# The turned softmax blocks of a neighbourhood attention: from DRAM and back on GpSimd's queue, or straight from SBUF to SBUF on SyncE's

## The chip, the cores and the metric

The kernel runs on one core of a Trainium2 chip. The metric is the device time of one execution in microseconds (us). Three runs of the kernel before gave 1162.82, 1160.19 and 1152.91 us, with the median at 1160.19 us.

## The reference, cut to what matters

One layer of a hybrid block in float32: a half-step SwiGLU, a mixer with two branches, a second half-step SwiGLU. There are 512 tokens (8 rows of a grid of 64 columns), 1024 features, 16 heads of 64, and a feed-forward width of 2816. Branch B of the mixer is the attention that the change touches: every token attends to the 8 rows by 16 columns around it. The reference computes it in 4 blocks of 16 query columns with 32 key columns each, and masks what lies outside the window.

```python
x = x + 0.5 * swiglu(rmsnorm(x), w_ffn1_gu, w_ffn1_down)
p = rmsnorm(x) @ w_in          # [rglru x | gelu gate | q | k | v | merge gate A | merge gate B]
A = (rglru(conv(px)) + rglru_backward(conv(px))) * gelu(pg)
s = einsum('bnqhd,brnkhd->bhnqrk', q, k) + rel_pos_bias     # q and k normalized, window masked
B = einsum('bnqhrk,brnkhd->bnqhd', softmax(s), v)
x = x + (sigmoid(gA) * A + sigmoid(gB) * B) @ w_out
x = x + 0.5 * swiglu(rmsnorm(x), w_ffn2_gu, w_ffn2_down)
```

## The kernel before, in words

**Precision and weights.** Every operand of a large product is split in two rounded parts, a high and a low one, and each product is three matmuls (high weight by high data, high by low, low by high: L171 to L174, and L831 to L833 where tokens are the rows of the result). A weight chunk is 128 x 1024 numbers, 512 KB, and gives 24 such matmuls. `load_w` (L159) makes it ready: SyncE (SP) issues the load into `wraw` at L163, ScalarE (ACT) casts it to `wh` at L145 (every other chunk of some stages is cast by VectorE, DVE, at L147), and DVE subtracts to get `wl` at L148. There are three buffers of `wraw` and four of `wh` and `wl`. So the load of a chunk waits for the split of the chunk three before it, and the split waits until TensorE (PE) is through with the chunk four before it.

**Stages.** The first feed-forward layer takes the time to some 390 us, then come the projections, the recurrence on GpSimd (POOL) and DVE, and the attention; the second feed-forward layer starts near 780 us. The middle of the program is woven: while PE works through the weight chunks of V (`wqkv`), of the three gates (`wg`, 24 chunks, named wg0 to wg23 here) and of W_out (`wout`, 8 chunks), pieces of the attention are put between them. The program's order is the starting point, a scheduler then sets the order on each engine, and what stands under `tc.high_priority()` is moved ahead.

**The attention.** `heads(hf, ...)` (L889) handles one half of the heads, hf = 0 or 1, in four feature tiles fi of two heads each. For each tile:
- `start(fi)` turns q and k with PE and splits them.
- `scores(fi, n2s)` handles pairs n2 of the four column blocks: PE makes the scores (L943) into PSUM tiles named `aux` and `acc`, DVE adds the bias tile `bm` and finds the row's extreme in one pass (L963), ACT takes the exponent (L970), DVE inverts the row sums (L972) and scales (L975). The weights stand in tiles `p`.
- `ship(fi, n2)` (L978) turns the weights so that keys come to lie on the partitions. DVE transposes inside each 32 x 32 block (L984 and L985) into `pt`, a tile of 128 x 4 x 7 x 32, of which there are two buffers. What is left is to swap whole blocks across partitions: block row j of column group i has to become block row i of column group j. Before, POOL stores `pt` to device memory (`pd`, L987, one transfer of 448 KB) and then issues four loads of 112 KB into `PT` (L991), which has four buffers.
- `apply(fi)` (L994) multiplies PT by V in 16 matmuls of 128 x 64 weights (L1005), the first 8 on the PT of n2 = 0, the last 8 on that of n2 = 1, and ACT copies the result to `att` (L1015).

In the first half (hf 0) a step of the weave is one pair of column blocks: 8 steps, and an apply comes two steps behind its last scores. In the second half (hf 1) a step is a whole feature tile: 4 steps with two ships each. So there are 16 ships and 8 applies. They are numbered here in order: ships 0 to 7 belong to hf 0 (0 and 1 to its fi 0), ships 8 to 15 to hf 1; apply 0 to 3 of a half are its fi 0 to 3.

**What else stands on the queues there.** On POOL's queue also run the loads of the bias tiles (`bm`, L885) and, between the halves, the store of V and its gather into tiles `va`, `ve`, `vs` (L860 to L873). On SP's queue run the weight loads (L163) and, late, `load_pairs` and the residual (`xd`, L1098). Behind the attention, `att` enters the merge at L1084 and L1085 (pair times att, plus A); the result is split into `yh` and `yl`, which are the data of the W_out chunks, and these lead to the second feed-forward layer.

Of the kernel before, what the change touches and what calls it, by code (L numbers as in the profile page):

```python
# [9 lines left out]
F32 = mybir.dt.float32  # L10
# [6 lines left out]
P = 128  # L17
# [9 lines left out]
NCB, QC = 4, 16  # L27
# [64 lines left out]
def block_kernel(ctx: ExitStack, tc, a, out):  # L92
    nc = tc.nc
# [7 lines left out]
    dram = ctx.enter_context(tc.tile_pool(name="dram", bufs=1, space=bass.MemoryType.DRAM))  # L101
# [6 lines left out]
    def nm(s):  # L108
        uid[0] += 1
        return f"{s}_{uid[0]}"  # L110
# [147 lines left out]
    def sub(out_, in0, in1, neg=False):  # L258

        if neg:  # L260
            nc.vector.scalar_tensor_tensor(out_, in0, -1.0, in1, ALU.mult, ALU.subtract)
        else:
            nc.vector.tensor_tensor(out_, in0, in1, ALU.subtract)
# [617 lines left out]
    def bias(g):  # L881

        for hp in range(2):
            bms[g, hp] = tiny.tile([P, 640], F32, tag="bm", bufs=4, name=nm("bm"))
            ld = nc.gpsimd.dma_start(bms[g, hp], a["rpb"][g * 2 + hp])  # L885
            if g == 0:
                after(ld, mark["xr"])

    def heads(hf, raws, st):  # L889
# [9 lines left out]
        for w in range(2):  # L899
            for j in range(NCB):  # L900
                t = raws[w][j].rearrange("p (h d) -> p h d", d=HD)
# [5 lines left out]
        def start(fi):  # L907
            fs = slice(fi * P, (fi + 1) * P)
            pq, pk = aux_t(), aux_t()
            for j in range(NCB):  # L910
                hold(nc.tensor.transpose(pq[:, j * P : (j + 1) * P], raws[0][j][:, fs], ident))
            for j in range(NCB):
                hold(nc.tensor.transpose(perm(pk)[:, j], raws[1][j][:, fs], ident))
            rev = lambda t: t.rearrange("p (j t) -> p j t", j=NCB)[:, :, ::-1]
            fwd = lambda t: t.rearrange("p (j t) -> p j t", j=NCB)
            qh, ql, kh, kl = (big_t(F32R, n=n) for n in ("qh", "ql", "kh", "kl"))
            nc.scalar.activation(rev(qh), fwd(pq), AF.Copy, scale=gq8)
            with tc.high_priority():
                nc.vector.scalar_tensor_tensor(rev(ql), fwd(pq), gq8, rev(qh.bitcast(F32)), ALU.mult, ALU.subtract)
            nc.scalar.activation(kh, pk, AF.Copy, scale=gk)  # L920
            with tc.high_priority():
                mark["kl"] = nc.vector.scalar_tensor_tensor(kl, pk, gk, kh.bitcast(F32), ALU.mult, ALU.subtract)
            grid = lambda t: t.rearrange("p (r c) -> p r c", r=ROWS)
            qk[fi] = qh, ql, grid(kh), grid(kl)
# [53 lines left out]
        def ship(fi, n2):  # L978

            outer, inner = soft.pop((fi, n2))  # L980
            t = big.tile([P, NCB, 7, 32], F32, tag="pt", bufs=2, name=nm("pt"))
            sub = lambda b, n: b[:, : n * P].rearrange("p (q c i) -> p q c i", q=n, i=32)
            to = t.rearrange("p c q i -> p q c i")
            nc.vector.transpose(to[:, 4:], sub(outer, 3))  # L984
            nc.vector.transpose(to[:, :4], sub(inner, 4))  # L985
            d = dram.tile([P, NCB, 7 * 32], F32, tag="pd", bufs=4, name=nm("pd"))
            nc.gpsimd.dma_start(d, t.rearrange("p c q i -> p c (q i)"))  # L987
            PT = big.tile([P, NCB, 7, 32], F32, tag="PT", bufs=4, name=nm("PT"))
            for j in range(4):
                q = slice(j * 32, (j + 1) * 32)  # L990
                nc.gpsimd.dma_start(PT[:, j].rearrange("p q i -> p (q i)"), d[q].rearrange("i c x -> c i x"))  # L991
            PTs[fi, n2] = PT.rearrange("p a q i -> p q a i")

        def apply(fi, behind=None):  # L994
            pv = aux_t()
            for n in range(NCB):
                PT = PTs[fi, n // 2]
                for half in range(2):
                    if n in EDGE:
                        vt = V[hf, "single" if half else "own", n]  # L1000
                    else:
                        vt = V[hf, (KSTART[n] + half * QC) // 8]
                    for h2 in range(2):
                        q = 4 + (1 if half else h2 * 2) if n in EDGE else h2 * 2 + half
                        mm = nc.tensor.matmul(  # L1005
                            pv[h2 * HD : (h2 + 1) * HD, n * P : (n + 1) * P],
                            vt[:, (fi * 2 + h2) * HD : (fi * 2 + h2 + 1) * HD],
                            PT[:, q],
                            start=half == 0, stop=half == 1)
                        if behind is not None:  # L1010
                            after(mm, behind)
                            behind = None
            at = big_t(n="att")
            with tc.high_priority():
                nc.scalar.activation(  # L1015
                    at.rearrange("p (j t) -> p j t", j=NCB), pv.rearrange("p (j t) -> p j t", j=NCB)[:, :, ::-1], AF.Copy)
            att[hf * 4 + fi] = at
# [7 lines left out]
        for i in range(len(units) + LC):  # L1025
            behind = None
            if i < len(units):
                fi, n2s = units[i]
                behind = scores(fi, n2s)
            if i >= LC and 1 in units[i - LC][1]:  # L1030
                apply(units[i - LC][0], behind)
            if i < len(units):
                for n2 in n2s:
                    ship(fi, n2)
                if 0 in n2s:
                    if fi < 3:
                        start(fi + 1)
                    if hf * 4 + fi + 1 < KT:
                        bias(hf * 4 + fi + 1)
            yield  # L1040
            if phase[0] == "g":
                yield
                yield
# [4 lines left out]
    for hf in range(2):  # L1048
        st = tiny.tile([P, 2, NCB, 8], F32, tag="st", name=nm("st"))
        raws = [qk_raw(0, hf, st), qk_raw(1, hf, st)]  # L1050
        v_get(hf)
        lanes["att"].append(heads(hf, raws, st))
        phase[0] = "t1" if hf == 0 else "g"
# [146 lines left out]
```

## Time and profile before

| what | value |
| --- | --- |
| median of three runs | 1160.19 us (1152.91 to 1162.82) |
| the profiled execution, its own time | 1158.95 us |
| its span in the trace | 1157.1 us |
| mean granted clock of TensorE | 0.979 of full speed |
| busy: PE / DVE / ACT / POOL | 1108.7 / 813.8 / 581.1 / 162.7 us |
| moved by the transfers | 175.93 MB in 63588 packets |

How to read it: the span is the time from the first to the last instruction of one execution, and what lies around it (1.85 us here) is the start and the end. An engine's busy time is the sum of its instructions. A row of the timeline shows the start, the duration, the engine, the source line, what was written from what, and in brackets the idle time of the engine just before it with what ended it. A row of the stages shows, for a stretch of the span, its length and then each engine's busy time with its count of instructions (PE, PE's weight loads, DVE, ACT, POOL), then the granted clock, the busy share of the 16 DMA engines, and GB/s. A row of the transfers shows what was written from what, the issuing queue, the count, the KB of one, and the median of the us from issue to landing.

### The profile page before, as it was taken

The numbers are of one execution on the slowest core, as the hardware profiler recorded it, in microseconds if no ns is written. First come the engines' busy times: TensorE is split into PE (matmuls) and PEld (weight loads), VectorE is DVE, ScalarE is ACT, GpSimd is POOL, SyncE is SP. The second block draws the span as 40 slices with busy tenths as digits, with TensorE's granted clock in tenths as the row PEclk, the third lists the DMA queues.
The fourth block names the chain that finished last, engine by engine and source line by source line (L and its number), as shares of the span: only waits on it lengthen the run. The fifth ranks groups of instructions, "written<-read, shape, count | busy, mean of one in ns | idle before, by whom it ended". The sixth has DMA issues, their size and how long they took to land.

```text
span 1157.1 us, 17667 instructions
## 1 busy us (share of the span) xinstructions
PE 1108.7 (96%) x6811; PEld 980.1 (85%) x6811; DVE 813.8 (70%) x1295; ACT 581.1 (50%) x873; POOL 162.7 (14%) x267
## 2 busy tenths in 40 slices
PE   9999999999999999998884999699999999999998
PEld 7899999988888778886773887578999999998887
DVE  7877777775836869997463589737877777875552
ACT  8554545553625778765242254435754545464340
POOL 0000000000000531422343003310000000000000
PEclk9999999999999999999896999889999999999999
DMA  8566666632423883845654436648666666653420
GB/s 265 150 159 159 163 152 169 164 117 91 135 75 106 230 247 107 237 126 161 170 160 114 135 109 199 195 129 217 177 153 159 163 153 168 153 166 98 128 85 36
DMA packets 63588, 175.93 MB, mean 152 GB/s; under 512 B 15120, under 2 KB 18960, under 8 KB 63504
## 3 DMA queue, kind: packets, MB, share of 16 engines
q1 hardware_dynamic: 39744, 118.31, 31.9%
q0 software_dynamic: 23184, 56.24, 22.9%
q8 instruction: 53, 0.87, 0.3%
q10 hardware_dynamic: 576, 0.26, 0.1%
q14 instruction: 31, 0.25, 0.1%
HBM read 150.53 MB, written 15.73 MB: 144 GB/s over the span
## 4 chain that ended last, share of the span: by engine, by line
PE 78%; issue 7%; DMA 6%; POOL 4%; DVE 3%; ACT 1%; ACTq 0%; POOLq 0%; DVEq 0%
PE acc L312 30%; PE acc L172 8%; PE acc L174 8%; PE acc L173 8%; PE aux L312 5%; DMA pd<-pt 4%; PE aux L173 4%; PE aux L172 3%; PE aux L174 3%; POOL PT L991 2%; PE acc L831 1%; PE acc L832 1%; PE acc L833 1%; DMA PT<-pd 1%; PE aux L742 1%
## 5 line engine op out<-in xcount | busy, mean ns | idle before, releaser
L145 ACT ACTIVATE wh<-wraw 128x1024 fp32r<-128x1024 f32 (+3 forms) x224 | 220.6, 988 | 322.2 <-issue 92.4
L148 DVE TENSOR_TENSOR wl<-wraw,wh 128x1024 fp32r<-128x1024 f32 (+3 forms) x236 | 267.3, 1137 | 100.7 <-ACT wh L145 97.7
L312 PE MATMUL acc<-s,wh 128*128 128x256 f32 x1280 | 232.1, 283 | 0.0
L312 PEld LDWEIGHTS acc<-s,wh 128*128 128x128 f32 x1280 | 199.7, 192 | 0.0
L312 PE MATMUL acc<-s,wl 128*128 128x256 f32 x640 | 181.1, 283 | 0.0
L312 PEld LDWEIGHTS acc<-s,wl 128*128 128x128 f32 x640 | 122.9, 192 | 0.0
L172 PE MATMUL acc<-xh,wh 128*128 128x512 f32 x272 | 109.0, 401 | 0.0
L174 PE MATMUL acc<-xh,wl 128*128 128x512 f32 x272 | 107.4, 395 | 0.0
L173 PE MATMUL acc<-xl,wh 128*128 128x512 f32 x272 | 107.3, 395 | 0.0
L312 PE MATMUL acc<-xl,wh 128*128 128x256 f32 x320 | 90.6, 283 | 0.0
L312 PE MATMUL acc<-xh,wl 128*128 128x256 f32 x320 | 90.6, 283 | 0.0
L312 PE MATMUL acc<-xh,wh 128*128 128x256 f32 x320 | 90.5, 283 | 0.0
L831 PE MATMUL acc<-wh,xh 128*128 128x512 f32 x192 | 76.4, 398 | 0.0
L832 PE MATMUL acc<-wh,xl 128*128 128x512 f32 x192 | 75.4, 393 | 0.0
L833 PE MATMUL acc<-wl,xh 128*128 128x512 f32 x192 | 75.2, 392 | 0.0
L148 DVE TENSOR_TENSOR hl<-h,hh 128x512 fp32r<-128x512 f32 x88 | 57.2, 686 | 21.7 <-PE aux L173 21.4
L172 PE MATMUL aux<-hh,wh 128*128 128x512 f32 (+1 forms) x181 | 69.9, 386 | 0.0
L173 PE MATMUL aux<-hl,wh 128*128 128x512 f32 (+1 forms) x181 | 69.9, 386 | 0.0
L174 PE MATMUL aux<-hh,wl 128*128 128x512 f32 (+1 forms) x181 | 69.9, 386 | 0.0
L173 PE MATMUL acc<-hl,wh 128*128 128x512 f32 (+1 forms) x176 | 67.9, 386 | 0.0
L174 PE MATMUL acc<-hh,wl 128*128 128x512 f32 (+1 forms) x176 | 67.9, 386 | 0.0
L172 PE MATMUL acc<-hh,wh 128*128 128x512 f32 (+1 forms) x176 | 67.9, 386 | 0.0
(223 smaller groups left out, 2322.2 us busy)
## 6 DMA issues: line engine op xcount, KB each, us to landing
wraw<-wqkv SPq DMA_DIRECT2D x24, 512.0 KB, 5.0
wraw<-wg SPq DMA_DIRECT2D x24, 512.0 KB, 3.9
wraw<-w1d SPq DMA_DIRECT2D x22, 512.0 KB, 3.7
wraw<-w2s SPq DMA_DIRECT2D x22, 512.0 KB, 4.2
pair<-w2s SPq DMA_DIRECT2D x22, 512.0 KB, 5.0
wraw<-w2d SPq DMA_DIRECT2D x22, 512.0 KB, 3.6
wraw<-w1s SPq DMA_DIRECT2D x18, 512.0 KB, 4.3
pair<-w1s SPq DMA_DIRECT2D x18, 512.0 KB, 5.6
```

The lines of the kernel that those rows point to most:

```text
L145: nc.scalar.activation(H, raw, AF.Copy)
L148: return nc.vector.tensor_tensor(L, raw, H.bitcast(F32), ALU.subtract)
L172: nc.tensor.matmul(ps, wh, xh, start=first, stop=False, skip_group_check=skip)
L173: nc.tensor.matmul(ps, wh, xl, start=False, stop=False, skip_group_check=skip)
L174: mark["mm"] = nc.tensor.matmul(ps, wl, xh, start=False, stop=last, skip_group_check=skip)
L312: mm = nc.tensor.matmul(o, w_[:, c], x_, start=first and m + k == 0 and w_ is H and x_ is xh_, stop=m + k == 4 and w_ is L, skip_group_che ...
L742: prev, mm = mm, nc.tensor.matmul(ps[d][b], W[w][o, c], X[x][o], start=x == 1, stop=w + x == 0)
L831: nc.tensor.matmul(pss[j], xh[kk][:, tj], H[:, s], start=kk == 0, stop=False)
L832: nc.tensor.matmul(pss[j], xl[kk][:, tj], H[:, s], start=False, stop=False)
L833: mark["mm"] = nc.tensor.matmul(pss[j], xh[kk][:, tj], L[:, s], start=False, stop=kk == KT - 1)
L991: nc.gpsimd.dma_start(PT[:, j].rearrange("p q i -> p (q i)"), d[q].rearrange("i c x -> c i x"))
```

## The change

`ship` no longer goes through device memory. The tile `pd`, its store and its four loads on POOL's queue are gone. In their place 16 transfers per ship are issued on SP's queue, each from `pt` straight into `PT`: 32 partitions of 224 numbers, 896 bytes a partition, 28 KB in all. And the whole ship, transposes and transfers, stands under `tc.high_priority()`.

```diff
             nc.vector.transpose(to[:, 4:], sub(outer, 3))
             nc.vector.transpose(to[:, :4], sub(inner, 4))
-            d = dram.tile([P, NCB, 7 * 32], F32, tag="pd", bufs=4, name=nm("pd"))
-            nc.gpsimd.dma_start(d, t.rearrange("p c q i -> p c (q i)"))
             PT = big.tile([P, NCB, 7, 32], F32, tag="PT", bufs=4, name=nm("PT"))
-            for j in range(4):
-                q = slice(j * 32, (j + 1) * 32)
-                nc.gpsimd.dma_start(PT[:, j].rearrange("p q i -> p (q i)"), d[q].rearrange("i c x -> c i x"))
+            for i in range(4):
+                for j in range(4):
+                    nc.sync.dma_start(PT[i * 32 : (i + 1) * 32, j], t[j * 32 : (j + 1) * 32, i])
             PTs[fi, n2] = PT.rearrange("p a q i -> p q a i")
...
                 for n2 in n2s:
-                    ship(fi, n2)
+                    with tc.high_priority():
+                        ship(fi, n2)
```

So 80 transfers on POOL's queue become 256 on SP's. The lines behind L985 move up by two: the new transfers are L989, the matmuls of apply L1003, and the merge L1083 and L1084.

Three places of the order of instructions are needed later. **SP's queue in hf 0.** `wraw` with its number is the load of a chunk of gate weights (the second to the seventh chunk from wg2 on), PT the transfers of a ship. Before:

```order
L163 DMA wraw_5789<-wg 128x1024
L163 DMA wraw_5821<-wg 128x1024
L163 DMA wraw_5916<-wg 128x1024
L163 DMA wraw_5960<-wg 128x1024
L163 DMA wraw_6041<-wg 128x1024
```

and with the change (the first row here is the chunk that stands second there):

```order
L163 DMA wraw_5871<-wg 128x1024
L989 DMA PT_5400<-pt_5397 32x224 x16
L163 DMA wraw_5976<-wg 128x1024
L989 DMA PT_5519<-pt_5516 32x224 x16
L989 DMA PT_5644<-pt_5641 32x224 x16
L163 DMA wraw_6020<-wg 128x1024
L163 DMA wraw_6111<-wg 128x1024
L163 DMA wraw_6143<-wg 128x1024
```

SP issues in this order and waits in it too. PT_5400 is ship 1, PT_5519 and PT_5644 are ships 2 and 3, and wraw_6020 is the fifth chunk from wg1 on, which now stands behind the 32 transfers of these two.

**DVE at the last two ships of hf 1** (14 and 15). `p` are the softmax weights, the brackets hold the semaphores on which the row waits: DMASW are those of POOL's transfers, DMAHW those of SP's, of which there are eight. Before:

```order
L984 STREAM_TRANSPOSE pt_7205<-p_7146 128x3x4x32 [waits DMASW5_49,DVE_49]
L1062 TENSOR_TENSOR pair_7231<-acc_7232,rstd_3726 128x512 [waits PE_49]
L148 TENSOR_TENSOR wl_7454<-wraw_7452,wh_7453 128x1024 [waits DMAHW7_49,Activation_49]
L975 TENSOR_SCALAR p_7149<-p_7149,rs_7117 128x256 [waits DVE_49]
...
L985 STREAM_TRANSPOSE pt_7205<-p_7147 128x4x4x32
...
L985 STREAM_TRANSPOSE pt_7215<-p_7149 128x4x4x32 [waits DMASW6_49,DVE_49]
```

and with the change:

```order
L148 TENSOR_TENSOR wl_7655<-wraw_7653,wh_7654 128x1024 [waits DMAHW0_49,Activation_49]
L984 STREAM_TRANSPOSE pt_7345<-p_7286 128x3x4x32 [waits DMAHW4_49,DMAHW5_49,DMAHW3_49,DMAHW6_49,DMAHW2_49,DMAHW7_49,DMAHW1_49,DMAHW0_49]
L985 STREAM_TRANSPOSE pt_7345<-p_7287 128x4x4x32
L984 STREAM_TRANSPOSE pt_7365<-p_7288 128x3x4x32 [waits DMAHW5_49,DMAHW7_49,DMAHW3_49,DMAHW1_49]
L985 STREAM_TRANSPOSE pt_7365<-p_7289 128x4x4x32
L1083 SCALAR_TENSOR_TENSOR pair_7391<-pair_7391,att_7442 128x512 [waits Activation_49]
```

The first transpose of a ship waited for one store of the ship two before it, and now for all 16 transfers of that ship; behind it on DVE stands a merge with `att`.

**PE at the last apply.** `acc_7354` is the second chunk of W_out before, `acc_7652` the fifth with the change, and `acc_7514` and the chunks after it the others, at their last data tile. Before:

```order
L174 MATMUL acc_7354<-yh_7113,wl_7357 128x512
L1005 MATMUL aux_7324<-PT_7210,va_5669 64x128 x2
L1005 MATMUL aux_7324<-PT_7210,ve_5670 64x128 x2
L1005 MATMUL aux_7324<-PT_7210,vs_5663 64x128 x2
L1005 MATMUL aux_7324<-PT_7210,vs_5665 64x128 x2
L172 MATMUL acc_7354<-yh_7227,wh_7356 128x512
...
L1005 MATMUL aux_7324<-PT_7220,vs_5665 64x128 x2
L1005 MATMUL aux_7324<-PT_7220,vs_5667 64x128 x2
```

and with the change:

```order
L174 MATMUL acc_7652<-yh_7446,wl_7655 128x512
L1003 MATMUL aux_7484<-PT_7348,va_5709 64x128 x2
L1003 MATMUL aux_7484<-PT_7348,ve_5710 64x128 x2
L1003 MATMUL aux_7484<-PT_7348,vs_5703 64x128 x2
L1003 MATMUL aux_7484<-PT_7348,vs_5705 64x128 x2
L1003 MATMUL aux_7484<-PT_7368,vs_5705 64x128 x2
...
L172 MATMUL acc_7514<-yh_7505,wh_7516 128x512
```

Before, 172 matmuls of W_out stand behind the last apply; with the change 108 do, the other 64 having moved ahead of it.

## The prediction

> **What bounds the kernel now.** I read the chain that ended last first, then the stages, then what PE waited for, and then the timeline of PE and of POOL around the longest of these waits. The page:
>
> ```profile
> span 1157.1 us, 17667 instructions
> ...
> PE acc L312 30%; PE acc L172 8%; PE acc L174 8%; PE acc L173 8%; PE aux L312 5%; DMA pd<-pt 4%; PE aux L173 4%; PE aux L172 3%; PE aux L174 3%; POOL PT L991 2%; PE acc L831 1%; PE acc L832 1%; PE acc L833 1%; DMA PT<-pd 1%; PE aux L742 1%
> ```
>
> Most of the chain is PE's, but `pd<-pt` with 4%, POOL's issue of `PT` with 2% and `PT<-pd` with 1% lie on it too: 7% of 1157 us, some 80 us, pass through the route that the change replaces. The stages, with PE's busy time in the second column behind the length:
>
> ```profile
> 560.00:625.00 65.00, 46.50 (x268) 37.51 (x267) 34.65 (x88) 22.75 (x43) 26.30 (x39) 0.88 0.61 166
> ...
> 700.00:770.00 70.00, 55.09 (x353) 44.23 (x350) 48.25 (x135) 28.06 (x72) 25.87 (x40) 0.90 0.62 182
> 800.00:1060.00 260.00, 260.00 (x2022) 253.56 (x2021) 201.15 (x253) 140.59 (x180) 19.02 (x22) 1.00 0.62 159
> ```
>
> In the second feed-forward layer PE is busy 260 us of 260 at full clock: nothing there can change. Time is lost between 500 and 770 us, where PE is idle for 18.5 of 65 us and its clock falls to 0.88. What it waits for, in total, times and longest:
>
> ```profile
> PE aux L1005 <- DMA PT<-pd: 41.4, 8, 10.4
> ```
>
> and the eight places:
>
> ```profile
> 552.54 1.12 PE L1005 MATMUL aux<-PT,vs 128*64 128x128 f32 x8 [8.38 <-DMA PT<-pd]
> 581.09 0.66 PE L1005 MATMUL aux<-PT,vs 128*64 128x128 f32 x8 [1.75 <-DMA PT<-pd]
> 616.64 0.70 PE L1005 MATMUL aux<-PT,va 128*64 128x128 f32 x4 [10.36 <-DMA PT<-pd]
> 626.48 1.12 PE L1005 MATMUL aux<-PT,vs 128*64 128x128 f32 x8 [7.86 <-DMA PT<-pd]
> 734.83 0.66 PE L1005 MATMUL aux<-PT,vs 128*64 128x128 f32 x8 [1.58 <-DMA PT<-pd]
> 744.93 0.44 PE L1005 MATMUL aux<-PT,va 128*64 128x128 f32 x4 [3.34 <-DMA PT<-pd]
> 751.58 1.12 PE L1005 MATMUL aux<-PT,vs 128*64 128x128 f32 x8 [5.32 <-DMA PT<-pd]
> 768.91 0.66 PE L1005 MATMUL aux<-PT,vs 128*64 128x128 f32 x8 [2.80 <-DMA PT<-pd]
> ```
>
> So 28.4 us are lost in hf 0 (the first four) and 13.0 in hf 1. Why PT is late stands on POOL's queue, here with the store and the four loads of ship 1, then the last of its transposes on DVE, then the landings of some transfers:
>
> ```profile
> 534.65 0.77 POOL L987 DMA_DIRECT2D pd<-pt  x1
> 543.51 2.03 POOL L991 DMA_DIRECT2D PT<-pd  x3 [8.09 <-DMA pd<-pt]
> 547.78 0.67 POOL L991 DMA_DIRECT2D PT<-pd  x1 [2.24 <-issue]
> ```
> ```profile
> 533.08 0.67 DVE L985 STREAM_TRANSPOSE pt<-p 128x512 f32<-128x512 f32 x1
> ```
> ```profile
> wraw<-wg SPq DMA_DIRECT2D x24, 512.0 KB, 3.9
> gate<-pair POOLq DMA_DIRECT2D x64, 128.0 KB, 5.3
> PT<-pd POOLq DMA_DIRECT2D x64, 112.0 KB, 4.1
> wraw<-w1gu SPq DMA_DIRECT2D x9, 64.0 KB, 2.6
> ```
>
> Ship 1 is turned at 533.75. Its store is issued at once, POOL waits for its landing (8.09 idle), and the last load is issued by 548.4 and lands some 4 later, just ahead of the 552.54 at which PE goes on: 18 us from transposed to usable, and 13.8 of POOL's queue, on which one ship follows the other. By the order of that queue, in the 616 and 626 rows it is the V gather that stands ahead of the ships.
>
> **What a stall costs.** From the first scores of hf 0 to those of hf 1 and on to the second feed-forward layer:
>
> ```profile
> 523.62 0.50 PE L831 MATMUL acc<-wh,xh 128*128 128x512 f32 x1
> 534.73 0.39 PE L943 MATMUL aux<-kl,qh 64*128 64x256 f32 x2
> 684.08 0.39 PE L943 MATMUL aux<-kl,qh 64*128 64x256 f32 x2
> 810.79 5.75 PE acc L312 x48
> ```
>
> (the last row is from the chain.) 48 matmuls fill 523.62 to 534.73, so a chunk of 24 takes 5.45 us with its gaps. The work of hf 0, which begins at 515.26, is 21 chunks, 8 scores of 0.95, 4 starts of 0.85 and 4 applies of 1.25 us: 130.5, and 684.08 - 515.26 is 168.8, so 38.3 are lost. From there to 810.79, 100.8 of work in 126.7 leave 25.9. Of these 64.2, the waits above are 41.4 and another is 1.9:
>
> ```profile
> 720.80 0.63 PE L913 MATMUL aux<-ident,qk 128*128 128x128 f32 x4 [1.86 <-DVE nmx L963]
> 722.13 0.63 PE L172 MATMUL acc<-xh,wh 128*128 128x512 f32 x1
> 725.62 0.40 PE L172 MATMUL acc<-xh,wh 128*128 128x512 f32 x1
> ```
>
> After that wait a matmul takes 0.63 instead of 0.40 for a few us. The other 20.9 us are this, 2.3 for each of nine stalls. An end to all waits for PT is then worth 41.4 + 8 x 2.3 = 59.8 us. (The Trainium skill, TensorE: Matmul & The Clock Gate, ties the low clock to an idle window of some 3.4 us; here 1.86 us of waiting brought it, and the trace decides.)
>
> **The new route's price.** 16 issues per ship on SP, one landing behind the last. No row shows a transfer of 32 partitions. For the issue:
>
> ```profile
> L163 SPq DMA_DIRECT2D wraw<-wg x24: 327/328/328, 512.1 to 695.4; - x24
> L1098 SPq DMA_DIRECT2D pair<-xd x8: 319/374/447, 744.4 to 774.2; - x8
> 4.22 2.80 SPq L446 DMA_DIRECT2D wraw<-w1gu  x6
> ```
>
> Each takes 0.33 to 0.37, in an unbroken run 2.80 / 6 = 0.47; I take 0.40. For the landing: between 2.6 (64 KB by SP, the nearest in size) and 3.9 (a weight load of SP's in this very stage); I take 3.2, as both share the queue. A ship is 6.4 + 3.2 = 9.6 us instead of 18, a pair of ships together 12.8 + 3.2 = 16.0. Bounds for a ship: 16 x 0.33 + 2.6 = 7.9, and 16 x 0.47 + 3.9 = 11.4. The transposes are the same instructions; POOL loses 80 issues, which frees the V gather. DRAM traffic falls from two passes of 448 KB per ship to none.
>
> **Part by part, hf 0.** Ship 1 is there at 533.75 + 9.6 = 543.4; PE comes for it at 552.54 - 8.38 = 544.2: the first stall goes, with under 1 us to spare (at the upper bound 1.0 us of it stays). The second and the two long ones go with several us to spare, since each ship waits for no gather and no other ship. What is late next is a weight load: SP issues in order, and the fifth gate chunk stands behind ships 2 and 3, whose last transpose is
>
> ```profile
> 560.27 0.67 DVE L985 STREAM_TRANSPOSE pt<-p 128x512 f32<-128x512 f32 x1
> 569.04 1.06 ACT L145 ACTIVATE wh<-wraw 128x1024 fp32r<-128x1024 f32 x1 [12.96 <-PE acc L173]
> 577.32 0.39 PE L943 MATMUL aux<-kl,qh 64*128 64x256 f32 x2
> ```
>
> It ends 8.4 earlier than here, at 552.6; 6.4 of issues to 559.0; the load 3.9 and more, to 563.2; ACT's cast 1.1; DVE's `wl` 1.2, to 565.5. That `wl` stands on DVE in the midst of the passes L963, with the next chunk's cast behind it, so the last pass ends near 567.2. PE's next scores (577.32 here) need the PSUM that it frees. They come 8.38 + 2.3 earlier, at 566.7. New stall 0.5 + 2.3 = 2.8. Without that load behind the ships it is nothing; at 0.47 an issue it is 4.
>
> **hf 1.** Here two ships come at once, and the transposes of a ship now wait for all 16 transfers of the one two before.
>
> ```profile
> 697.15 0.67 DVE L985 STREAM_TRANSPOSE pt<-p 128x512 f32<-128x512 f32 x1
> 710.80 0.67 DVE L985 STREAM_TRANSPOSE pt<-p 128x512 f32<-128x512 f32 x1
> 733.10 0.67 DVE L985 STREAM_TRANSPOSE pt<-p 128x512 f32<-128x512 f32 x1
> ```
>
> Ships 8 and 9 are turned by 697.8, and the first of the two some 3 us sooner by my estimate, so their last issue is near 708 and their last landing near 711 to 712, and the transposes of 10 and 11 wait about 0.9 (a loss of 0.9 on DVE). These are ready at 713, landed at 713 + 16 = 729, before PE comes (734.83 - 1.58 = 733.3). Ships 12 and 13: 735, landed at 751.0. By counting the matmuls ahead of it PE comes for apply 2, which the order has moved behind more of W_out's, at 752.4: nothing. Ships 14 and 15 wait to 751.0 for `pt`, are turned by 753.4 and landed at 769.4; apply 3 would start at 766.3 by the same count: stall 3.1 + 2.3 = 5.4. Behind that apply PE now has nothing that does not need its result, since the 64 other matmuls have moved ahead:
>
> ```profile
> 770.36 0.60 ACT L1015 ACTIVATE att<-aux 128x512 f32<-128x512 f32 x1 [6.24 <-PE aux L1005]
> 772.50 0.63 ACT L145 ACTIVATE yh<-pair 128x512 fp32r<-128x512 f32 x1 [1.54 <-DVE pair L1085]
> ```
>
> From 770.36 to 773.13 are 2.8 us, a bubble with 2.3 of slow clock: 5.1. The split before it and the start of the second feed-forward layer have less cover: 3 together, between 0 and twice that. The 1.86 stays.
>
> **The sum.** 59.8 gained, less 2.8 in hf 0 and 0.9 + 5.4 + 5.1 + 3.0 = 14.4 in hf 1: 42.6. From the profiled execution's 1158.95 (median 1160.2, so 1.2 under it) that is **1116 us**. With 0.33 an issue and 2.0 a landing (the least of L446's) a pair takes 12.6, the waits for PT vanish, 9 of the new loss stay, and 1108 comes out; with nothing lost 1099. With 0.47 and 3.9 a pair takes 18.9: the new losses grow by about 3 per pair from ship 12 on, 1 at ship 1 and 1 to 4 in hf 0, which gives 1128. The likeliest's own range is 1100 to 1135.
>
> **Rivals.** (1) *Landings set the pace, not issues.* SP's transfers take eight semaphores in turn, and each waits for the one eight before it to land. At an issue of 0.40 eight issues take 3.2, so a landing beyond 3.2 spreads them. At 4.1 (the 112 KB row) a pair is 3 x 4.1 + 3.2 + 4.1 = 19.6 and the gain some 19: 1140. At 5.3 (`gate<-pair`, the one row from SBUF to SBUF) a ship is 13.8 and a pair 24.4: ship 1 is there at 547.6, leaving 3.4 of the first stall, the weight loads are 4 to 8 late at three places, and ships 12 to 15 come 8 and 17 later: hf 0 keeps some 23, hf 1 loses as much: 1159, no change. From there on the change is slower; at 6.7, 1178. For it: 256 small transfers share 16 engines with 512 KB loads. Against: those 5.3 are POOL's queue with 128 KB, and SP's 64 KB took 2.6. (2) *Weight loads late behind ships in hf 1*, where 32 issues hold SP for 12.8 us while PE eats a chunk in 5.45, with three buffers ahead: two chunks late by 5 take a third of the gain: 1130 to 1145. Against: of the W_out chunks five are issued before the last ships. (3) *Other waits show up* behind those removed (bias tiles, V gather, DVE's softmax): half the gain, 1138. (4) *The transfers run one after the other.* 16 x 2.6 = 42 us a ship, against the 13.8 of ship 1 on POOL: 256 x 2.6 = 666 us of queue in a stretch of 270, so some 1400 us. Against it: six issues in 2.80 us while one lands in 2.6, so they overlap.
>
> The Trainium skill (DMA: Bandwidth & Descriptors, Rules for kernel authors) speaks against the change: many small transfers are to be coalesced, below 64 KB one mostly pays overhead, and transfers to disjoint partitions serialize because all share the 16 engines. By that a ship of 16 pieces of 28 KB would pay 16 overheads, which is rival 4 if they are paid in turn and the forecast if they overlap. The rows bear out the second.
>
> **How the numbers follow.** Forecast 0.60; rival 1 0.20 (of it 0.06 near 1140, 0.05 within 1%, 0.09 slower); rivals 2 0.10 and 3 0.07, both mostly faster; rival 4 0.03. About 1% is what a measurement can tell from no change here: 1148.6 to 1171.8. Faster 0.60 + 0.06 + 0.13 = 0.79; within 1% 0.05 + 0.04 = 0.09; slower 0.12. The range reaches from 1099, nothing lost, to 1150, which holds rivals 2 and 3 and the near end of 1; I leave out what is beyond.
>
> **What would show it.** Right: PE's waits for PT at the four places of hf 0 gone, one at the last apply of 2 to 5 us; SP's issues 0.35 to 0.45 apart; `PT<-pt` landing in 2.6 to 3.9; the clock of 560 to 625 near 0.97. Wrong: landings above 5 us, PE waiting for `wl` or for L963 behind late weight loads at several places, or DVE's L984 waiting long for transfers.

## The result, and the profile after

The change made the kernel slower, by 0.7%: a median of 1166.06 us in 18 runs (1162.54 to 1168.13), against 1157.88 for the kernel before in its 18 runs beside them, a ratio of 1.0071 (95% interval 1.0053 to 1.0090). Forecast were 1116 us, some 43 faster.

The profiled execution took 1163.24 us, with a span of 1161.4. It still moves the data once instead of twice, and the waits for PT are down from 41.4 to 19.4 us. The page's chain and the waits say where the time went instead:

```profile
span 1161.4 us, 17878 instructions
...
PE 84%; SPq 8%; DMA 4%; DVE 2%; issue 1%; ACT 1%; DVEq 0%; ACTq 0%
PE acc L312 29%; SPq L989 8%; PE acc L172 8%; PE acc L173 8%; PE acc L174 7%; PE aux L312 5%; PE acc L831 4%; PE aux L173 3%; PE aux L172 3%; PE aux L174 3%; PE acc L832 3%; PE acc L833 3%; PE aux L742 1%; DMA wraw<-wg 1%; DMA PT<-pt 1%; PE aux L1003 1%
```
```profile
PE aux L1003 <- DMA PT<-pt: 19.4, 4, 9.6
DVE pt L984 <- DMA PT<-pt: 18.7, 3, 8.1
...
PE aux L913 <- DVE nmx L963: 8.1, 1, 8.1
PE aux L943 <- DVE nmx L963: 3.0, 1, 3.0
```

The transfers themselves are 1% of the chain, but `SPq L989`, SyncE's act of issuing them, is 8%: some 93 us. The groups of SP's issues, and the landings:

```profile
L989 SPq DMA_DIRECT2D PT<-pt x256: 507/589/1830, 524.7 to 766.4; - x128
```
```profile
PT<-pt SPq DMA_DIRECT2D x256, 28.0 KB, 1.9
```

One issue takes 0.589 us in the median, and with the step to the next and some longer ones it comes to 0.65 to 0.67 a transfer (20.79 to 21.39 us for the 32 of a pair, below). A landing takes 1.9 from the start of its issue. SP's timeline around the second half of the heads:

```profile
673.77 21.39 SPq L989 DMA_DIRECT2D PT<-pt  x32
695.27 0.52 SPq L163 DMA_DIRECT2D wraw<-wg  x1
696.22 0.81 SPq L163 DMA_DIRECT2D wraw<-wout  x2
698.44 21.31 SPq L989 DMA_DIRECT2D PT<-pt  x32
719.85 1.48 SPq L163 DMA_DIRECT2D wraw<-wout  x3
723.02 20.79 SPq L989 DMA_DIRECT2D PT<-pt  x32
744.14 1.84 SPq L1097 DMA_DIRECT2D pair<-xd  x4
746.09 20.93 SPq L989 DMA_DIRECT2D PT<-pt  x32
767.28 0.84 SPq L1097 DMA_DIRECT2D pair<-xd  x2
```

From 673.77 to 768 the queue stands still for some 4 us in all. A pair of ships holds it for 20.8 to 21.4 us, and pairs follow at 24.1 (746.09 - 673.77 is 72.3, over three). The pause between two pairs is that of the next pair's transposes on DVE, and the loads fit into it:

```profile
695.96 1.24 DVE L984 STREAM_TRANSPOSE pt<-p 128x384 f32<-128x384 f32 x2 [5.57 <-DMA PT<-pt]
720.75 1.03 DVE L984 STREAM_TRANSPOSE pt<-p 128x384 f32<-128x384 f32 x2
744.43 0.58 DVE L984 STREAM_TRANSPOSE pt<-p 128x384 f32<-128x384 f32 x1 [8.11 <-DMA PT<-pt]
```

Each of these begins within 1.1 us of the end of a pair's issues (695.16, 719.75 and 743.81), as the last transfers of that pair land. So the first transpose of a pair did not wait only for the ship two before it, as the text on the order of instructions above has it: ship 12's issues ended at 733.67 and a landing takes 1.9 us, yet ship 14's first transpose began at 744.43, when ship 13 was landing. The stages and PE's waits:

```profile
500.00:560.00 60.00, 54.29 (x300) 43.91 (x298) 45.99 (x105) 29.41 (x64) 6.25 (x10) 0.94 0.38 107
560.00:625.00 65.00, 61.73 (x337) 50.81 (x336) 37.54 (x94) 27.28 (x51) 15.05 (x22) 0.97 0.57 166
...
700.00:770.00 70.00, 48.49 (x275) 39.74 (x277) 35.35 (x94) 21.26 (x51) 0.00 (x0) 0.88 0.32 93
800.00:1060.00 260.00, 253.29 (x1964) 247.80 (x1964) 196.43 (x248) 137.87 (x177) 17.94 (x21) 0.97 0.61 155
```
```profile
549.66 1.12 PE L1003 MATMUL aux<-PT,vs 128*64 128x128 f32 x8 [5.71 <-DMA PT<-pt]
578.00 0.39 PE L943 MATMUL aux<-kl,qh 64*128 64x256 f32 x1 [2.97 <-DVE nmx L963]
707.77 1.09 PE L913 MATMUL aux<-ident,qk 128*128 128x128 f32 x4 [8.13 <-DVE nmx L963]
744.45 0.44 PE L1003 MATMUL aux<-PT,va 128*64 128x128 f32 x4 [3.12 <-DMA PT<-pt]
768.07 0.70 PE L1003 MATMUL aux<-PT,va 128*64 128x128 f32 x4 [9.65 <-DMA PT<-pt]
774.61 0.79 PE L172 MATMUL acc<-yh,wh 128*128 128x512 f32 x1 [2.86 <-ACT yh L145]
811.32 0.48 PE L312 MATMUL aux<-xh,wh 128*128 128x256 f32 x1 [2.23 <-ACT xh L196]
825.19 0.80 PE L312 MATMUL acc<-s,wh 128*128 128x256 f32 x2 [2.95 <-ACT p L353]
```

The stage 560 to 625 is nearly filled now, as forecast. But the stage 700 to 770 lost 6.6 us of PE's work against before, and the second feed-forward layer, which had no gap, lost 6.7 us at its start. Split at the second half's first matmul of scores into `acc`, the balance is plain. Before, and after:

```profile
684.92 0.28 PE L943 MATMUL acc<-kl,qh 64*128 64x256 f32 x2
664.86 0.30 PE L943 MATMUL acc<-kl,qh 64*128 64x256 f32 x2
```

Hf 0 came 20.1 us earlier. From there to the end of the span it was 1157.1 - 684.92 = 472.2 before, and 1161.4 - 664.86 = 496.5 now: 24.3 lost in hf 1 and behind it. Net 4.3 us slower, which is the difference of the spans.

### The profile page after: what moved, and what is told of

Its sections match the earlier page's. It is cut to its first block, busy times and chain, and to the rows that moved or that the text cites. A ratio compares the mean times of both kernels' runs of the same rounds, so it can differ in the third digit from the quotient of the medians.

```text
span 1161.4 us, 17878 instructions
## 1 busy us (share of the span) xinstructions
PE 1115.8 (96%) x6811; PEld 987.1 (85%) x6811; DVE 813.4 (70%) x1295; ACT 580.8 (50%) x873; POOL 109.7 (9%) x187
## 4 chain that ended last, share of the span: by engine, by line
PE 84%; SPq 8%; DMA 4%; DVE 2%; issue 1%; ACT 1%; DVEq 0%; ACTq 0%
PE acc L312 29%; SPq L989 8%; PE acc L172 8%; PE acc L173 8%; PE acc L174 7%; PE aux L312 5%; PE acc L831 4%; PE aux L173 3%; PE aux L172 3%; PE aux L174 3%; PE acc L832 3%; PE acc L833 3%; PE aux L742 1%; DMA wraw<-wg 1%; DMA PT<-pt 1%; PE aux L1003 1%
## 5 line engine op out<-in xcount | busy, mean ns | idle before, releaser
L312 PE MATMUL acc<-s,wh 128*128 128x256 f32 x1280 | 236.1, 286 | 3.9 <-ACT p L353 3.0
L312 PEld LDWEIGHTS acc<-s,wh 128*128 128x128 f32 x1280 | 202.6, 195 | 4.7 <-ACT p L353 3.2
L148 DVE TENSOR_TENSOR wl<-pair,wh 128x1024 fp32r<-128x1024 f32 x40 | 48.8, 1222 | 28.3 <-ACT wh L145 28.3
```

The source lines that it names most:

```text
L148: return nc.vector.tensor_tensor(L, raw, H.bitcast(F32), ALU.subtract)
L312: mm = nc.tensor.matmul(o, w_[:, c], x_, start=first and m + k == 0 and w_ is H and x_ is xh_, stop=m + k == 4 and w_ is L, skip_group_che ...
```

## The experiments

Theory A: what costs is SP's issue time, some 0.66 us a transfer from one to the next instead of the 0.40 of the prediction. The rivals: the new order of instructions that the priority brings (B), or landings and shared transfer engines (C). All ratios below are to the kernel before, run beside each.

### Half of the transfers on another queue; one half of the heads alone; no priority; issues by themselves

**split_pool**, the even split, moves every other transfer to GpSimd's queue:

```diff
-                    nc.sync.dma_start(PT[i * 32 : (i + 1) * 32, j], t[j * 32 : (j + 1) * 32, i])
+                    (nc.gpsimd if (i + j) % 2 else nc.sync).dma_start(PT[i * 32 : (i + 1) * 32, j], t[j * 32 : (j + 1) * 32, i])
```

> Of the 16 transfers of a ship, the 8 with i + j odd are issued on GpSimd's queue instead of SyncE's, all else as in the changed kernel. Theory A (the cost is SyncE's issue time: in the changed kernel 16 issues took 10.2 to 10.7 us per ship, 21.4 per pair, against 6.4 and 12.8 in the prediction): each queue now spends some 5.3 us per ship, so a ship comes in 5.3 + 2 to 5 and SyncE's weight loads are held half as long; that is near the prediction's own 9.6 and 16.0, and 1115 to 1135 us come out. Rival B (the new order of instructions in the second half costs the time, not the transfers): no faster than 1155. Rival C (landings or shared transfer engines set the pace): landings grow and the time stays at 1160 or more.

Measured: 1113.45 us, ratio 0.9688 (0.9651 to 0.9726), a little below theory A's range. Of PE's waits in the attention two are left, and the stages are full:

```profile
500.00:560.00 60.00, 60.00 (x342) 49.12 (x341) 49.32 (x108) 30.68 (x66) 24.29 (x44) 1.00 0.47 144
560.00:625.00 65.00, 64.93 (x371) 52.39 (x370) 43.65 (x102) 30.33 (x54) 30.18 (x52) 1.00 0.56 163
...
700.00:770.00 70.00, 67.27 (x361) 55.45 (x358) 51.78 (x100) 36.29 (x64) 15.90 (x30) 0.98 0.69 194
800.00:1060.00 260.00, 260.00 (x1883) 247.43 (x1882) 187.65 (x230) 128.78 (x165) 14.54 (x17) 1.00 0.55 148
```
```profile
688.74 0.63 PE L913 MATMUL aux<-ident,qk 128*128 128x128 f32 x4 [1.69 <-DVE nmx L963]
709.93 1.07 PE L1003 MATMUL aux<-PT,vs 128*64 128x128 f32 x8 [2.73 <-DMA PT<-pt]
```

The same 256 transfers over the same transfer engines, with landings of 2.5 to 2.6 instead of 1.9, come in time once two queues issue them. Rival C is out. Rival B's 1155 was missed by far too, but the order shifts a little with the route, so the next runs are needed for it.

**hf0_only** keeps the new route in hf 0 and puts the old one back in hf 1:

```diff
+            if hf == 1:
+                d = dram.tile([P, NCB, 7 * 32], F32, tag="pd", bufs=4, name=nm("pd"))
...
+                return
...
-                    with tc.high_priority():
+                    with tc.high_priority() if hf == 0 else nullcontext():
```

> The new route and its priority for the first half of the heads only; the second half goes through device memory on GpSimd's queue as before. The changed kernel reached the first scores of the second half 20 us sooner than the kernel before and then lost 24 us. Theory A and rival B: the 20 stay and the 24 do not come, 1138 us (1132 to 1144). If the second half's loss is instead the price of running sooner (weights not there whatever the route): above 1150.

Measured: 1138.24 us, ratio 0.9899 (0.9872 to 0.9925), a gain of 12 us in its own runs rather than 20. In its profile PE still waited for PT in hf 1 by the old route, 5.3 us at the longest and 14.1 in four places. The loss of the changed kernel is thus in hf 1.

**no_prio** is the changed kernel with `ship` out of `tc.high_priority()`.

> The new route as in the changed kernel, but the ship no longer stands under high priority. Theory A: the queue's time per ship stays 10.7 us, so the time stays within 10 us of the changed kernel (1155 to 1175), as only the places of the ships on the queues move. Rival B (the priority's order costs the second half its 24 us): 1140 to 1146.

Measured: 1160.20 us, ratio 1.0091 (1.0055 to 1.0126). Rival B is out as the main cause: without the priority the loss is the same. In its profile the first transpose of the second pair began at 690.27, while ship 9 was still being issued, and pairs followed at 21.2 us instead of 24.1. PE still waited 27.6 us for PT, in seven places, so the pause between pairs is not what decides either.

**issue_menu** adds 54 tiny transfers to SP's queue, which read constants or inputs and write a scratch tile:

```diff
+    kinds = [(n, "s") for n in (8, 16, 32, 64, 128)] + [(32, "from"), (128, "from"), (32, "to"), (128, "to")]
+    for r, (n, kind) in enumerate(kinds):
+        for c in range(6):
...
+                nc.sync.dma_start(scr[:n, cs], ones[P - n :, c * 8 : (c + 1) * 8])
```

> The changed kernel with 54 extra transfers of 32 bytes a partition on SyncE's queue, in a scratch tile that nothing reads: SBUF to SBUF with 8, 16, 32, 64 and 128 partitions, device memory to SBUF with 32 and 128, SBUF to device memory with 32 and 128, six of each. Only the issue time of each kind counts, not the time of the kernel. If the issue time goes with the partitions or the bytes: it falls well below 0.59 us for 8 partitions. If it is a fixed price of a transfer between two places in SBUF: 0.55 to 0.6 for all five, and 0.32 to 0.45 for those from or to device memory. If it is crossing partitions: less for 128 partitions, the only one of the five that does not cross.

Measured, from SBUF to SBUF with 8, 32 and 128 partitions, from device memory, and to it, one row of each kind:

```profile
13.22 0.63 SPq L1128 DMA_DIRECT2D scr<-ones  x1
45.91 0.59 SPq L1128 DMA_DIRECT2D scr<-ones  x1
55.52 0.60 SPq L1128 DMA_DIRECT2D scr<-ones  x1
59.67 0.43 SPq L1130 DMA_DIRECT2D scr<-rpb  x1
65.14 0.42 SPq L1132 DMA_DIRECT2D dscr<-ones  x1
```

The price is all but fixed: 0.59 to 0.60 us between two places in SBUF in an unbroken run, for 32 to 128 partitions and whether they cross or not (0.63 with 8), for 32 bytes a partition as for 896. With device memory at one end it is 0.42 in an unbroken run and down to 0.32 behind a pause. So the rows of SP's queue in the kernel before, all of them with device memory at one end, could not show the price of the new transfer there.

### How many on which queue

**split_12_4** leaves 12 of 16 on SP's queue (`nc.gpsimd if (i + j) % 4 == 3 else nc.sync`).

> 12 transfers of a ship on SyncE's queue, the 4 with (i + j) mod 4 = 3 on GpSimd's. SyncE then spends 12 x 0.65 = 7.8 us per ship and 15.6 per pair, with landings of 2.5 us a pair is there after 18. The changed kernel's pair takes 21.4 + 1.9 = 23.3, the even split's 10.7 + 2.5 = 13.2 at the most. Theory A (time follows the queue's time per ship): between the two kernels, 1125 to 1145; a straight line between 1113 at 8 and 1166 at 16 gives 1140, the prediction's own working, which puts most of the loss beyond 16 us a pair, 1125. If any weight load behind ships is what costs, however long: above 1155.

Measured: 1117.93 us, ratio 0.9725 (0.9695 to 0.9754). That is below theory A's range: the prediction's working, at 1125, was nearer than the straight line.

**all_pool** puts all 16 on GpSimd's queue (`nc.gpsimd.dma_start`).

> All 16 transfers of a ship on GpSimd's queue, none on SyncE's. In the split kernel GpSimd issued 8 in 4.0 to 4.3 us, 0.50 each, so a ship takes 8.0 to 8.6 and a pair 16 to 17, plus 2.5 to land: 18.5 to 19.7 a pair, and no weight load stands behind a ship; V's gather and the bias tiles do. Theory A: some ships of the second half are late, the loads never, 1115 to 1135. If it is the mere 16 on one queue that costs, as on SyncE's: 1155 or more.

Measured: 1159.75 us, ratio 1.0088 (1.0058 to 1.0119), far above theory A's range. GpSimd's timeline in hf 1, the first row, the end of the second pair and the start of the third, and the last pair:

```profile
682.99 2.47 POOL L989 DMA_DIRECT2D PT<-pt  x5 [3.11 <-issue]
...
711.79 9.80 POOL L989 DMA_DIRECT2D PT<-pt  x20 [0.23 <-DMA PT<-pt]
728.13 13.24 POOL L989 DMA_DIRECT2D PT<-pt  x27 [6.54 <-PE aux L1003]
...
749.93 0.50 POOL L989 DMA_DIRECT2D PT<-pt  x1 [4.68 <-issue]
751.30 15.23 POOL L989 DMA_DIRECT2D PT<-pt  x31 [0.87 <-issue]
```

An issue takes 0.50 there, and a pair 16.0 to 17.1 us. But between pairs the queue stands still for 4.7 to 6.5 us, until DVE has turned the next pair (its transposes began at 702.82, 725.96 and 748.21, as the pair before had landed). So pairs follow at 22.3, and the 128 transfers take from 682.99 to 766.53. No weight load stood behind a ship, and yet the kernel is as slow as the changed one. Late ships are enough for a loss of this kind; held weight loads are not needed. Only a part of it lies in these rows, though: hf 1 began at 673.59 here, 20.6 us later than in the even split.

**pool_21** lengthens that by cutting 5 transfers of a ship in two.

> As all on GpSimd's queue, but 5 of the 16 transfers of a ship are cut in two halves of 16 partitions, so that 21 issues of 0.50 take 10.5 us: a ship comes as late as in the changed kernel, while SyncE's weight loads are free of it. It tells the two shares of the loss apart. If late ships are the most of it: 1145 to 1162, with PE's waits for PT in the second half as in the changed kernel. If weight loads held behind ships are the most: 1135 or less.

Measured: 1176.56 us, ratio 1.0232 (1.0201 to 1.0262). Slower than the range, on the side of late ships: pairs follow at 25.9 us, and PE waited 12.5 us for PT at the last apply.

**split_no_prio** is the even split without the priority.

> The even split over both queues (1113 us) without the high priority of the ships. The changed kernel without it stood at 1160 against 1166, in other runs. If the priority is worth nothing once the ships are quick: 1108 to 1120. If it is what gets the ships onto the queues in time (without it they stand behind more weight loads in the second half): 1125 or more.

Measured: 1115.47 us, ratio 0.9703 (0.9677 to 0.9728). The priority is worth nothing that these intervals tell apart.

### Where in the second half

**tail_split** splits only ships 14 and 15 of the changed kernel (`(i + j) % 2 and hf == 1 and fi == 3`).

> The changed kernel, but the last two ships (14 and 15) alone are split evenly over SyncE's and GpSimd's queues. In the changed kernel PE waited 9.6 us for these two, then 2.9 for the merge behind them and 6.7 at the start of the second feed-forward layer, some 26 us with the slow clock. If these come from the two ships being late: 1138 to 1145. If the order behind the last apply (it still stands near the end of W_out, with 116 matmuls of W_out behind it instead of 108) and the earlier ships carry them: only the first wait shrinks, 1150 to 1160.

Measured: 1152.97 us, ratio 1.0001 (0.9981 to 1.0020). PE's last wait for PT fell from 9.65 to 0.33, as PE's timeline shows, and the rest stayed. The last two ships are a part, not the cause.

**tail_sp** is the reverse: the even split, with ships 14 and 15 on SP alone.

> The even split (1113 us) for all ships but the last two, which have all 16 transfers on SyncE's queue. Theory A: these two come some 11 us later, of which the order hides a part (the last apply stands 50 rows further behind): 1118 to 1130. If the last two carry the loss of the changed kernel: 1135 or more.

Measured: 1112.84 us, ratio 0.9656 (0.9626 to 0.9687): no loss at all, less than expected. One slow pair on a queue that is up to date cost nothing here: PE had no wait at its apply, which has 140 matmuls of W_out behind it instead of 177, so that 37 more stand ahead of it.

**split_act** and **split3** use ScalarE's queue, for every other transfer and for a third of them (`(nc.sync, nc.gpsimd, nc.scalar)[(i + j) % 3]`).

> As the even split, but the second half of the transfers goes on ScalarE's queue instead of GpSimd's: 128 issues of some 0.59 us, 75 us of ScalarE's time in a stretch in which it casts weights and takes exponents. If only the queue's time per ship counts: 1108 to 1118, as with GpSimd. If ScalarE's casts come late by it: 1120 to 1140.

> The transfers of a ship over three queues: 6 on SyncE's, 5 on GpSimd's, 5 on ScalarE's. A ship then takes 6 x 0.65 = 3.9 us of issues instead of 5.2, a pair 7.8. In the even split PE still waited 2.7 us for PT and 1.7 for a pass of VectorE, some 9 us with the slow clock. If these are late ships: 1104 to 1110. If ScalarE's time costs what is gained: 1111 to 1120.

Measured: 1144.11 us, ratio 0.9932 (0.9911 to 0.9953), and 1124.48, ratio 0.9757 (0.9731 to 0.9784). Both are slower than the even split and than their ranges. An issue takes 0.60 on ScalarE, and in split_act its casts and exponents also stood behind transfers: PE waited 13.3 us for one VectorE result that came from a ScalarE copy behind 16 of them. A queue of an engine that is needed for other work is no free queue.

### A rate or a step

PE's first scores of the four feature tiles of hf 1 in the even split:

```profile
653.03 0.28 PE L943 MATMUL acc<-kl,qh 64*128 64x256 f32 x2
666.63 0.28 PE L943 MATMUL acc<-kl,qh 64*128 64x256 f32 x2
682.96 0.28 PE L943 MATMUL acc<-kl,qh 64*128 64x256 f32 x2
697.67 0.28 PE L943 MATMUL acc<-kl,qh 64*128 64x256 f32 x2
```

PE uses a pair of ships every (697.67 - 653.03) / 3 = 14.9 us. Two runs were to tell whether the excess of SP's time over that adds up.

**split_14_2** leaves 14 of 16 on SP (`nc.gpsimd if (i, j) in ((0, 3), (3, 0)) else nc.sync`); **hf1_split** has all 16 on SP in hf 0 and the even split in hf 1 (`(i + j) % 2 and hf == 1`).

> 14 transfers of a ship on SyncE's queue, 2 on GpSimd's. In the second half of the heads PE comes for a feature tile every 14.9 us (first scores of the four tiles in the even split: 652.2, 665.9, 682.2, 696.9). A pair of ships holds SyncE for 32 x 0.66 = 21.4 us in the changed kernel, with the loads between them 24.1 from pair to pair; here 28 x 0.66 = 18.5 and 20.5 with the loads; at 12 of 16, 15.6 and 17.6. Theory D (a rate: each pair's excess over 14.9 adds up over three intervals): 28 us lost at 16, 8 at 12, 17 here, so 1127 to 1140. Rival E (a step: the order of the last apply, with too little behind it, costs the most): it stands with the changed kernel's, 1150 or more, or with the 12 of 16, 1122 or less.

> All on SyncE's queue in the first half of the heads, the even split in the second. In the first half a ship holds the queue for 10.7 us and PE comes for one every 17 to 19 us, so by theory D only what the changed kernel lost there remains: its second half began at 664.1, that of the even split at 652.2, and from there the even split took 458.4 to its end: 664.1 + 458.4 + 1.8 = 1124 us (1119 to 1129). By rival F (the second half's loss comes from what the first half left behind on the queues): 1140 or more.

Measured: 1139.01 us, ratio 0.9904 (0.9877 to 0.9931), and 1127.65, ratio 0.9798 (0.9765 to 0.9831). Both lie in their ranges, split_14_2 near the upper end. In the profiles, from the first scores into `acc` of hf 1 to the end of the span (the pair's time is the median of the four pairs in SP's timeline in that half, for 8 of 16 it is 16 x 0.66; no_prio, the changed kernel without the priority, is set beside them):

| kernel | on SP in hf 1 | pair on SP, us | to the end, us | lost against the even split |
| --- | --- | --- | --- | --- |
| split_pool | 8 of 16 | 10.6 | 1110.6 - 653.03 = 457.6 | |
| hf1_split | 8 of 16 | 10.6 | 1125.7 - 667.78 = 457.9 | 0.3 |
| split_12_4 | 12 | 15.6 | 1116.5 - 650.97 = 465.5 | 7.9 |
| split_14_2 | 14 | 18.4 | 1136.4 - 653.21 = 483.2 | 25.6 |
| no_prio | 16 | 20.7 | 1155.3 - 665.55 = 489.8 | 32.2 |
| the changed kernel | 16 | 21.1 | 1161.4 - 664.86 = 496.5 | 38.9 |
| the kernel before | none | | 1157.1 - 684.92 = 472.2 | 14.6 |

Under 14.9 us a pair nothing is lost; just above it a little; then some 5 to 6 us for each further us of a pair. That is a rate, with a threshold near the point where SP's time per pair passes PE's. The excess over 14.9 alone, three times over, would be 2.1, 10.5 and 18.6 us at 12, 14 and 16 of 16, a quarter to a half of what is lost. The rest is put down to the slow clock behind each wait, the end of the attention and, but for no_prio, the pause between pairs; these shares were not measured apart. What a late last apply does to the start of the second feed-forward layer is in it: those stalls appear in the profiles of the changed kernel, all_pool, pool_21, tail_split and split_14_2, and in all five the last apply stands with only 108 to 123 matmuls of W_out behind it, against 145 in split_12_4, which has none of those stalls. But the loss does not need them: no_prio has 171 behind its last apply and none of those stalls, and it lies on the same line.

On GpSimd's queue pool_21, with pairs of some 22 us, lost 45.4 us in the same measure (1174.3 - 671.29 = 503.0), which fits the line. all_pool, with pairs of some 17 us, lost 28.3 (1159.5 - 673.59 = 485.9) and does not: the queue's own time is not all of it there, since pairs followed only at 22.3.

And hf 0, where a ship has some 18 us, is indifferent to what hf 1 does: hf1_split began hf 1 at 667.78, the changed kernel at 664.86. It is not free of the price, though. The even split began hf 1 at 653.03, 12 to 15 us sooner, while a ship's 10.1 to 11.3 us on SP are well under 18.

## Why the prediction was wrong

**The step that failed** is in "The new route's price": "Each takes 0.33 to 0.37, in an unbroken run 2.80 / 6 = 0.47; I take 0.40." It is some 0.66 from one issue to the next. The bounds came from rows with device memory at one end, and their upper one, 0.47, was taken for an end of the range though no row showed a transfer inside SBUF on SP. The landing was off the other way, 1.9 instead of 3.2, which is worth little, since a pair pays it once and the issue 32 times: 12.8 + 3.2 = 16.0 became 21.1 + 1.9 = 23.0. In the prediction's own working (rival 1) a pair of 19.6 us gives 1140 and one of 24.4 gives 1159; 23.0 lies on the straight line between them near 1153, an estimate. That is 37 of the 47 us by which the forecast missed the 1163 of the profiled execution; the rest is left to the waits below that were sized too small. The mechanism was about right; the price was not.

**Rival 1** named nearly the right size for the wrong reason. It has landings beyond 3.2 us spread the issues; the landings were 1.9 and the issues set the pace by themselves. **Rival 4** and the page of the Trainium skill quoted beside it (DMA: Bandwidth & Descriptors, Rules for kernel authors), by which small transfers mostly pay overhead, were put aside because six issues in 2.80 us overlap with landings. They do overlap, but the overhead of issuing is paid in turn, 16 times a ship, and that decided. By that rule, 28 KB at 0.66 us, this case agrees: the price did not depend on the bytes.

**Hf 0** was forecast to gain 28.4 + 4 x 2.3 - 2.8 = 34.8 us and gained 20. The first stall did not go: ship 1's issues began only at 535.69, behind the 10.2 us of ship 0 and a load, took 10.7, and PE waited 5.71. The fifth gate chunk was late just where it was said, at the next scores, by 2.97 instead of 0.5. The other three stalls went.

**Hf 1** was forecast to gain 13.0 + 4 x 2.3 - 14.4 = 7.8 and lost 24.3. The bubble behind the last apply was 2.86 where 2.8 was predicted; the wait of that apply 9.65 instead of 3.1; the start of the second feed-forward layer 6.7 instead of a share of 3. Of the transposes, which wait for earlier transfers to land, 0.9 was expected. Here the size was off most: DVE waited 18.7 us in three places, 5.57 of it at the second pair, and PE 8.13 for the passes behind that.

"Nothing there can change", said of the second feed-forward layer, was wrong too: the inputs of its first matmuls came late.

**What was right**: the route bounded the attention, and its removal is worth about what was said where the issues keep up. The even split's profiled execution took 1112.35 us against 1158.95, 46.6 less where 42.6 were forecast, and its median is 37 us under that of the kernel before in the same runs. That even split has 10.6 us of issues a pair on SP, less than the 12.8 of the prediction, so the two gains agree only roughly by the same working.

## What to carry to other kernels

Before moving work to a queue, multiply the number of transfers by the issue time of that very kind (both ends, that engine) and set the product, with what else holds up the queue between units, against the time in which the consumer uses one unit. Above it every unit adds to the loss: 21.1 us against 14.9 lost 39 us in hf 1, and 10.6 lost nothing. Below it the queue keeps up, but a unit that is needed at once still comes late, as ship 1 of hf 0 did. Where it does not fit, two queues of engines with little else to do can turn the same change from a loss to a gain: here from 1.0071 to 0.9688. Whether more buffers of `pt`, or fewer and larger transfers, would do so too was not tried.

## What the runs showed of the hardware

- An issue on SyncE's queue between two places in SBUF took 0.59 to 0.60 us in an unbroken run for 32 to 128 partitions (0.63 for one with 8), with 32 or 896 bytes a partition, and some 0.51 behind a pause; with device memory at one end 0.32 to 0.43 as a rule. On GpSimd's queue the SBUF transfer took 0.50, on ScalarE's 0.60.
- A 28 KB transfer inside SBUF landed in 1.9 us on SyncE's queue alone (median of 256), and in 2.5 to 2.6 when SyncE's and GpSimd's queues issued them in turn; with SyncE's and ScalarE's in turn it was 1.9 and 2.0.
- On GpSimd's queue alone a pair's 32 transfers took 16.0 to 17.1 us, on SyncE's 20.8 to 21.4; the quicker issue was lost again in this kernel, as the queue stood still for 4.7 to 6.5 us between pairs.
- Behind PE's waits the granted clock fell: 0.88 from 700 to 770 us with the change, against 0.98 in the even split.
